# Keys stored a second time in the order of tokens modulo 4, and the triangular products of two heads issued in turn

## The chip, the cores and the metric

One core of a Trainium2 chip runs one program. The metric is device time in microseconds from the program's start to its end; the time of a kernel is the median of its runs.

## What is computed

One decoder layer of 2048 tokens and width 1024, all in float32. Half of the width goes through eight RWKV-7 heads, half through eight attention heads of 64 channels, then an output projection, a layer norm, a mixture of experts and another layer norm. Of this the change touches the attention and the RWKV heads:

```python
DIL_PATTERNS = ((128, 1), (512, 4), (2048, 16))

def dilated_branch(q, k, v, rel_bias, window, dil):
    ...
    def subsample(t):
        t = t.reshape(B, L, dil, H, Dh).transpose(0, 2, 3, 1, 4)
    ...
    logits = jnp.einsum('bdhnqc,bdhnkc->bdhnqk', qs, kb) * (HEAD_DIM ** -0.5) + bias[None, None, :, None]
```

Each head attends three times: in blocks of 128 consecutive tokens, in blocks of 128 tokens that are 4 apart, and in blocks of 128 tokens that are 16 apart. In the first two a block also sees the block before it in the same residue class. The three results are combined by a softmax over their log-sums. The RWKV heads run a recurrence over the tokens, which the kernel computes in chunks of 128 tokens.

## The kernel before

The work runs in stages: `project` (L203) makes all projections, `mixers` (L889) runs RWKV and attention side by side, then come the output projection, the router and the experts. The change touches the first two.

**Projection.** Each product of 128 output channels and 512 tokens is 24 matmuls. For queries and keys (kinds 3 and 4) the sum in PSUM is split into a high part `oh` (L277, ScalarE) and a low part `ol` (L278, VectorE), and both are written to scratch arrays `qs` and `ks` in DRAM (L280) in the order of tokens. The staging tiles have two tags, "a" and "b", of two buffers each. The key chunks are the last that are projected; beside them run the preparation steps of RWKV (`rwkv_prep`, L558), which read and write DRAM too.

**Attention.** `attn_streams` (L968) goes through four head pairs, `hp`, and for each through the patterns n in the order 0, 2, 1. Queries and keys of a head pair lie in two resident tiles, `Q` and `KK`, which `load_qk` (L994) fills in four groups of 512 tokens; `close` (L1017) is called when four blocks are done, loads the values for the next pass and, after the last pattern, the next head pair's queries and keys. A matmul's stationary operand is a block of queries and its moving operand are the keys. `toks` (L1030) gives the access pattern of both: consecutive tokens for n = 0, every 4th word for n = 1, every 16th for n = 2. A block with a block before it needs two products of 256 columns for each head (L1059); one without, a single product that covers high and low part (L1062). Three streams take blocks in turn.

**RWKV.** For 16 rounds and two units each, `rwkv_front` (L648), `rwkv_inverse` (L702) and `rwkv_state` (L799) form triangular products from two heads of 64 channels. The heads lie on partitions 0 to 63 and 64 to 127, so a product of one head uses half of the array's rows. Each writes a PSUM buffer of its own out of the two that a unit has. The helper `triangles` (L643) makes one head's products for a front or an inverse (L646); a state's are made at L818.

**Order.** `weave` (L139) merges the streams by costs written into them as `yield _pe(900)` and the like. The compiler's scheduler then orders each engine's instructions once more by times of its own, so the order of an engine's queue is that of the built program and not that of the lines. An engine works its queue in that order. All loads named here are issued from the queue of SP.

## Time and profile before

| what | value |
|---|---|
| median of 3 runs | 3293.04 us (3287.47 to 3302.23) |
| profiled execution | 3298.42 us, its span 3296.5 us |
| TensorE (PE) busy | 2947.2 us, 89% of the span |
| VectorE (DVE) busy | 2111.6 us, 64% |
| ScalarE (ACT) busy | 1532.7 us, 46% |
| GpSimd (POOL) busy | 674.0 us, 20% |
| DMA | 533.18 MB, mean 162 GB/s |
| chain that ended last | VectorE 1%, issue 1%: the last norm only |

PE is the time of matmuls, PEld that of weight loads, which overlap matmuls. A float32 matmul appears as two records, one of the float32r type as one. The duration of a record covers its whole way through the array, so what a matmul costs its successor is read as the distance between starts. A line such as `L1059 PE MATMUL ... x432 | 115.5, 396 | 14.9` says: 432 records, busy 115.5 us together, 396 ns on average, and 14.9 us of idle time before them, with what ended it. In a timeline the columns are start, length, engine, line, operation, tiles and count, and in brackets the idle time before.

### The profile page before, as it was taken

Reading aid. Unit: us, or ns where it says so; the run is one execution under the profiler, and the core shown is the slowest. Engines: PE = TensorE matmul, PEld = TensorE weight load, DVE = VectorE, ACT = ScalarE, POOL = GpSimd, SP = SyncE. Lnnn points to the kernel's source line nnn. Section 1 sums busy time; section 2 is a strip of 40 time slices with the busy share of each in tenths; the row PEclk is TensorE's granted clock in tenths of the full one; section 3 lists DMA queues with packets and bytes.
Section 4 is the critical chain, followed back from the end, with each engine's and each line's share of the span. In section 5 each row is a group of like instructions: output and inputs, shape, how many; then the busy total and the mean of one; then the engine's idle time right before and its main releaser. Section 6 shows DMA issues by size and latency. Waiting matters only on the chain. (4 is left out here: it accounts for less than half of the span.)

```text
span 3296.5 us, 49200 instructions
## 1 busy us (share of the span) xinstructions
PE 2947.2 (89%) x16686; PEld 2350.5 (71%) x16687; DVE 2111.6 (64%) x4698; ACT 1532.7 (46%) x3650; POOL 674.0 (20%) x673
## 2 busy tenths in 40 slices
PE   7989768999898999998997899899999999998880
PEld 6766656777677777777785677788777777776560
DVE  4997224687555655755748587663577877775756
ACT  3444112465354544444443333411467777765642
POOL 0442000154110212112103122313011111112216
PEclk9999888999889998898997899999999999999895
DMA  5213342598816335235214344233499999996845
GB/s 164 80 58 99 91 73 81 155 287 254 199 45 127 101 84 121 74 78 129 67 38 139 101 150 156 101 136 92 145 309 306 324 314 313 327 300 220 295 128 207
DMA packets 364110, 533.18 MB, mean 162 GB/s; under 512 B 92376, under 2 KB 204736, under 8 KB 363840
## 3 DMA queue, kind: packets, MB, share of 16 engines
q1 hardware_dynamic: 333240, 463.94, 45.0%
q0 software_dynamic: 14208, 45.74, 5.8%
q10 hardware_dynamic: 16408, 20.33, 1.9%
q8 instruction: 134, 2.20, 0.3%
q14 instruction: 120, 0.98, 0.1%
HBM read 402.40 MB, written 128.06 MB: 161 GB/s over the span
## 5 line engine op out<-in xcount | busy, mean ns | idle before, releaser
L1701 DVE TENSOR_TENSOR wl<-raw,wh 128x512 fp32r<-128x512 f32 x768 | 478.1, 682 | 86.3 <-ACT wh L1700 85.8
L1700 ACT CAST wh<-raw 128x512 fp32r<-128x512 f32 x768 | 417.9, 622 | 11.8 <-DMA raw<-in_w_up_dram 10.6
L198 PE MATMUL ps<-xh,wh 128*128 128x512 f32 x640 | 263.4, 412 | 0.4 <-ACT xh L322 0.4
L199 PE MATMUL ps<-xl,wh 128*128 128x512 f32 x640 | 259.6, 406 | 1.0 <-DVE xl L323 1.0
L200 PE MATMUL ps<-xh,wl 128*128 128x512 f32 x640 | 258.7, 404 | 0.0
L1078 ACT ACTIVATE pe<-pe,ms 128x256 f32<-128x256 f32 (+1 forms) x384 | 175.5, 459 | 145.8 <-DVE ms L1075 143.6
L1830 POOL DMA_INDIRECT acc<-ysb,ix x48 | 95.7, 1994 | 624.1 <-ACT ysb L1829 401.7
L198 PE MATMUL pe<-wh,XX 128*128 128x512 f32 x480 | 198.7, 414 | 4.2 <-ACT wh L1700 4.2
L199 PE MATMUL pe<-wl,XX 128*128 128x512 f32 x480 | 191.1, 398 | 2.6 <-DVE wl L1701 2.6
L200 PE MATMUL pe<-wh,XX 128*128 128x512 f32 x480 | 189.7, 395 | 0.0
L198 PEld LDWEIGHTS ps<-xh,wh 128*128 128x128 f32 x640 | 125.3, 196 | 34.3 <-issue 2.8
L199 PEld LDWEIGHTS ps<-xl,wh 128*128 128x128 f32 x640 | 125.2, 196 | 30.3 <-DVE xl L323 2.5
L200 PEld LDWEIGHTS ps<-xh,wl 128*128 128x128 f32 x640 | 124.6, 195 | 29.6
L1098 PE MATMUL po<-pe,V 128*64 128x128 f32 x1200 | 126.0, 308 | 10.7 <-DVE O L1110 7.5
L1059 PE MATMUL pl<-KK,Q 128*128 128x256 f32 x432 | 115.5, 396 | 14.9 <-DMA KK<-ks 6.9
L1084 PE MATMUL pl<-eye,pe 128*128 128x128 f32 x600 | 124.1, 299 | 3.7 <-ACT pe L1078 3.2
L198 PE MATMUL pb<-gh,XH 128*128 128x512 f32 x320 | 126.4, 395 | 0.0
L199 PE MATMUL pb<-gl,XH 128*128 128x512 f32 x320 | 125.6, 392 | 0.0
L200 PE MATMUL pb<-gh,XL 128*128 128x512 f32 x320 | 125.1, 391 | 0.0
L1745 PE MATMUL pe<-wh,XX 128*128 128x512 f32 x288 | 119.7, 416 | 5.4 <-ACT wh L1700 5.4
L198 PE MATMUL pa<-woh,YH 128*128 128x512 f32 x256 | 111.3, 435 | 11.7 <-DVE h L1349 6.8
L1746 PE MATMUL pe<-wl,XX 128*128 128x512 f32 x288 | 118.5, 412 | 2.9 <-DVE wl L1701 2.9
(415 smaller groups left out, 7602.3 us busy)
## 6 DMA issues: line engine op xcount, KB each, us to landing
raw<-in_w_gate_dram SPq DMA_DIRECT2D x128, 512.0 KB
raw<-in_w_up_dram SPq DMA_DIRECT2D x128, 512.0 KB
raw<-in_w_down_dram SPq DMA_DIRECT2D x128, 512.0 KB
pk<-pk SPq DMA_DIRECT2D x32, 512.0 KB
pk_t<-pk SPq DMA_DIRECT2D x32, 512.0 KB
KK<-ks SPq DMA_DIRECT2D x64, 256.0 KB
wr<-in_w_in_dram SPq DMA_DIRECT2D x48, 256.0 KB
rkk<-rkk SPq DMA_DIRECT2D x32, 384.0 KB
```

The lines of the kernel that those rows point to most:

```text
L198: mm(out, lh, rh, start=first, stop=False)
L199: mm(out, lh, rl, start=False, stop=False)
L200: mm(out, ll, rh, start=False, stop=last)
L1059: mm(pl[:, h], q, toks(KK[:, m, h], n, prev, 2), start=m == 0, stop=m == 1)
L1078: nc.scalar.activation(pe[:, h, w], pe[:, h, w], AF.Exp, bias=m_[h], scale=-1.0, accum_out=s_[h])
L1084: nc.tensor.transpose(pt[:, h, b], pe[:, h, b * P:(b + 1) * P], self.c("eye"))
L1098: mm(o[h * 64:(h + 1) * 64, j], vb[:, h * 64:(h + 1) * 64], tt[:, h, b], start=b == kb[0], stop=b == 1)
L1700: nc.scalar.copy(wh[:, c], raw[:, c])
L1701: nc.vector.tensor_tensor(out=wl[:, c], in0=raw[:, c], in1=wh.bitcast(F32)[:, c], op=ALU.subtract)
L1745: mm(ps, L[:, 0:P], wh, start=first, stop=False)
L1746: mm(ps, L[:, 0:P], wl, start=False, stop=last)
L1830: nc.gpsimd.indirect_dma_start(out=self.acc, out_offset=bass.IndirectOffsetOnAxis(ap=ix[0:r, e, b:b + 1], axis=0), in_=ysb[0:r], in_offset ...
```

## The change

Keys (kind 4) are also written to a third array, `ks4`, in which every group of 512 tokens is sorted by token modulo 4: ScalarE copies `oh` and `ol` with a step of 4 into two further tiles of the tags "a" and "b", and each is written with a DMA. After the first pattern of a head pair `close` loads `ks4` over the keys, group by group; the patterns n = 2 and n = 1 read keys from that order (`keys`), with consecutive words for n = 1 and, for n = 2, runs of 32 words with a step of 4. Queries are read as before (`queries`). No product of n = 2 is placed before the first pattern's last group is closed. In the RWKV functions the products of the two heads are written in turn, into two PSUM buffers that are taken together, and the costs given to `weave` change from twice 860, 430 and 900 to once 900, 500 and 950.

```diff
@@ -203,7 +203,8 @@
     def project(self):
         nc, tc, I = self.nc, self.tc, self.I
         x = I["x"][0]
-        self.qs, self.ks = (self.scratch(n, (4, 2, P, S)) for n in ("qs", "ks"))
+
+        self.qs, self.ks, self.ks4 = (self.scratch(n, (4, 2, P, S)) for n in ("qs", "ks", "ks4"))
         self.va = self.scratch("va", (S, DH))
         self.rkk = self.scratch("rkk", (3, DH, S))
         self.rv = self.scratch("rv", (DH, S))
@@ -278,6 +279,11 @@
                         nc.vector.scalar_tensor_tensor(out=ol, in0=ps, scalar=sc, in1=oh.bitcast(F32), op0=ALU.mult, op1=ALU.subtract)
                         for n, o in enumerate((oh, ol)):
                             nc.sync.dma_start((self.qs, self.ks)[kind - 3][cc, n, :, cols], o.bitcast(F32))
+                        if kind == 4:
+                            for n, (o, tag) in enumerate(((oh, "a"), (ol, "b"))):
+                                o4 = st.tile([P, BT], F32, name="o4", tag=tag)
+                                nc.scalar.copy(o4.rearrange("p (d i) -> p d i", d=4), o.bitcast(F32).rearrange("p (i d) -> p d i", d=4))
+                                nc.sync.dma_start(self.ks4[cc, n, :, cols], o4)
                         yield
                         return
                     sh = st.tile([P, BT + 1], F32, name="sh", tag="a")
@@ -640,10 +646,12 @@
         nc.sync.dma_start(v, self.rv[u * P:(u + 1) * P, q * W:(q + 1) * W])
         pp.update(ta=pk[:, 0:W], rt=pk[:, W:2 * W], bk=pk[:, 2 * W:].rearrange("p (c m t) -> p c m t", c=2, m=2), v=v, rho=self.rho[:, u, q])
 
-    def triangles(self, out, pp, h, m):
-        hs = slice(h * 64, (h + 1) * 64)
+    def triangles(self, outs, pp, m):
+
         for c in range(2):
-            self.nc.tensor.matmul(out[:, c], pp["ta"][hs, c * P:(c + 1) * P], pp["bk"][hs, c, m], start=True, stop=True)
+            for h in range(2):
+                hs = slice(h * 64, (h + 1) * 64)
+                self.nc.tensor.matmul(outs[h][:, c], pp["ta"][hs, c * P:(c + 1) * P], pp["bk"][hs, c, m], start=True, stop=True)
 
     def rwkv_front(self, n, pps, last):
 
@@ -655,13 +663,13 @@
         self.busy = True
         C, Dg = T("C", [P, 2, 4, 32], 1), T("Dg", [P, 2, 4, 16], 1)
         AB = T("AB", [P, 2, 2, 2, P], ROUNDS)
+        yield _pe(900)
+        pa = [self.rps[0].tile([P, BT], F32, name="ps0", tag="ps0").rearrange("p (a c s) -> p a c s", a=2, c=2) for _ in range(2)]
+        for i, pp in enumerate(pps):
+            self.triangles([pa[h][:, i] for h in range(2)], pp, 0)
         for h in range(2):
-            yield _pe(860)
-            pa = self.rps[0].tile([P, BT], F32, name="ps0", tag="ps0").rearrange("p (a c s) -> p a c s", a=2, c=2)
-            for i, pp in enumerate(pps):
-                self.triangles(pa[:, i], pp, h, 0)
             yield _dve(4 * P)
-            nc.vector.tensor_tensor(out=AB[:, :, h], in0=pa, in1=self.c("low").unsqueeze(1).unsqueeze(1).to_broadcast([P, 2, 2, P]), op=ALU.mult)
+            nc.vector.tensor_tensor(out=AB[:, :, h], in0=pa[h], in1=self.c("low").unsqueeze(1).unsqueeze(1).to_broadcast([P, 2, 2, P]), op=ALU.mult)
         for i, pp in enumerate(pps):
             pp["AB"] = AB[:, i]
             for d in range(0, P, 32):
@@ -709,12 +717,12 @@
             yield None
         AB, ta = pp["AB"], pp["ta"]
         AW = T("AW", [P, 2, 2, 192])
+        yield _pe(500)
+        pa = [ps()[:, 0:2 * P].rearrange("p (c s) -> p c s", c=2) for _ in range(2)]
+        self.triangles(pa, pp, 1)
         for h in range(2):
-            yield _pe(430)
-            pa = ps()[:, 0:2 * P].rearrange("p (c s) -> p c s", c=2)
-            self.triangles(pa, pp, h, 1)
             yield _dve(2 * P)
-            nc.vector.tensor_tensor(out=AW[:, h, :, 64:192], in0=pa, in1=self.c("low").unsqueeze(1).to_broadcast([P, 2, P]), op=ALU.mult)
+            nc.vector.tensor_tensor(out=AW[:, h, :, 64:192], in0=pa[h], in1=self.c("low").unsqueeze(1).to_broadcast([P, 2, P]), op=ALU.mult)
         yield _pe(215)
         pt = ps()[:, 0:2 * P].rearrange("p (c s) -> p c s", s=P)
         for c in range(2):
@@ -810,12 +818,13 @@
         rt, v = ([pp[m][:, cs] for cs in col] for m in ("rt", "v"))
         bk = [pp["bk"][:, c] for c in range(2)]
         MJ, MK = T("MJ", [P, 2, 2, P]), T("MK", [P, 2, P])
-        for h in range(2):
-            yield _pe(900)
-            pr = ps().rearrange("p (c k s) -> p c k s", c=2, k=2)
-            for c in range(2):
-                for m in range(2):
-                    mm(pr[:, c, m], bk[c][H[h], m], rt[c][H[h]], start=True, stop=True)
+        yield _pe(950)
+        prs = [ps().rearrange("p (c k s) -> p c k s", c=2, k=2) for _ in range(2)]
+        for c in range(2):
+            for m in range(2):
+                for h in range(2):
+                    mm(prs[h][:, c, m], bk[c][H[h], m], rt[c][H[h]], start=True, stop=True)
+        for h, pr in enumerate(prs):
             yield _dve(2 * P)
             nc.vector.tensor_tensor(out=RB[:, h, :, 0:P], in0=pr[:, :, 0, :], in1=self.c("upi").unsqueeze(1).to_broadcast([P, 2, P]), op=ALU.mult)
             yield _dve(2 * P)
@@ -991,13 +1000,15 @@
             skew = src[:, P - 1:P - 1 + P * (L - 1)].rearrange("h (i l) -> i h l", l=L - 1)[:, :, 0:2 * P]
             nc.sync.dma_start(bias[k % 2], skew)
 
-        def load_qk(hp, g):
+        def load_qk(hp, g, ks=None):
+
             cols = slice(g * BT, (g + 1) * BT)
             for n in range(2):
                 half = slice(n * 64, (n + 1) * 64)
-                nc.sync.dma_start(Q[half, :, cols], self.qs[hp, n, :, cols].rearrange("(h c) t -> c h t", h=2))
+                if ks is None:
+                    nc.sync.dma_start(Q[half, :, cols], self.qs[hp, n, :, cols].rearrange("(h c) t -> c h t", h=2))
                 for m in range(2):
-                    nc.sync.dma_start(KK[half, m, :, cols], self.ks[hp, m, :, cols].rearrange("(h c) t -> c h t", h=2))
+                    nc.sync.dma_start(KK[half, m, :, cols], (ks or self.ks)[hp, m, :, cols].rearrange("(h c) t -> c h t", h=2))
 
         def load_v(hp, n, g):
             vcols = slice(hp * P, (hp + 1) * P)
@@ -1024,18 +1035,32 @@
                 load_v(*passes[k + 1], f)
                 if n == 1:
                     load_qk(hp + 1, f)
+                elif n == 0:
+                    load_qk(hp, f, self.ks4)
             if g == 3:
                 load_bias(k + 2)
 
-        def toks(t, n, blk, count):
+        def queries(t, n, blk):
+
+            t = t.bitcast(F32R)
+            if n == 0:
+                return t[..., blk * P:(blk + 1) * P]
+            if n == 1:
+                b, d_ = blk // 4, blk % 4
+                return t[..., b * BT + d_:(b + 1) * BT:4]
+            return t[..., blk::16]
+
+        def keys(t, n, blk, count):
 
             t = t.bitcast(F32R)
             if n == 0:
                 return t[..., blk * P:(blk + count) * P]
             if n == 1:
                 b, d_ = blk // 4, blk % 4
-                return t[..., b * BT + d_:(b + count) * BT:4]
-            return t[..., blk::16]
+                t = t.rearrange("p (b d i) -> p b d i" if len(t.shape) == 2 else "p m (b d i) -> p m b d i", b=4, d=4)
+                return t[:, b:b + count, d_] if len(t.shape) == 4 else t[:, :, b, d_]
+            t = t.rearrange("p m (b d i e) -> p m b d i e", b=4, d=4, e=4)
+            return t[:, :, :, blk % 4, :, blk // 4]
 
         def blocks(s, k):
             hp, n = passes[k]
@@ -1050,16 +1075,20 @@
                 if prev is not None and prev < 0:
                     prev = None
                 two = prev is not None
+                while n == 2 and (hp, 0, 3) not in closed:
+                    yield None
                 yield _pe(450 if two else 230)
                 pl = self.aps.tile([P, 2, 2 * P], F32, name=f"pl{s}", tag=f"pl{s}")
                 for h in range(2):
-                    q = toks(Q[:, h], n, blk, 1)
+                    q = queries(Q[:, h], n, blk)
                     if two:
                         for m in range(2):
-                            mm(pl[:, h], q, toks(KK[:, m, h], n, prev, 2), start=m == 0, stop=m == 1)
+                            kk = keys(KK[:, m, h], n, prev, 2)
+                            mm(pl[:, h].rearrange("p (b i) -> p b i", b=2) if n else pl[:, h], q, kk, start=m == 0, stop=m == 1)
                     else:
 
-                        mm(pl[:, h].rearrange("p (m i) -> p m i", m=2), q, toks(KK[:, :, h], n, blk, 1), start=True, stop=True)
+                        out = pl[:, h].rearrange("p (m i) -> p m i", m=2)
+                        mm(out.rearrange("p m (b i) -> p m b i", b=4) if n == 2 else out, q, keys(KK[:, :, h], n, blk, 1), start=True, stop=True)
                 w = slice(0 if two else P, 2 * P)
                 pe = first(f"pe{s}", [P, 2, 2 * P])
                 if hp not in stats:
```

The built order shows what becomes of this. First, TensorE's queue at a state's triangular products; `ps0_...` are PSUM buffers, one for each head, and each row of `x4` is one head. Before:

```order
L1084 MATMUL pl2_10451<-eye_60,pe2_10393 128x128 x2
L818 MATMUL ps0_9839<-pk_t_9277 128x128 x4
L1098 MATMUL po_7275<-pe0_10076,V_7274 64x128 x2
L1062 MATMUL pl0_10222<-KK_7271,Q_7270 128x256 x2
L818 MATMUL ps0_9859<-pk_t_9277 128x128 x4
L1098 MATMUL po_7275<-pe1_10105,V_7274 64x128 x2
L1062 MATMUL pl1_10309<-KK_7271,Q_7270 128x256 x2
```

and in the changed program:

```order
L826 MATMUL ps0_9982<-pk_t_9452 128x128 x4
L862 MATMUL ps1_10472<-RB1_10137,WF1_10378 64x192 x4
L826 MATMUL ps0_9983<-pk_t_9452 128x128 x4
L879 MATMUL ps1_10522<-vt1_10244,MK1_10139 128x128
L1091 MATMUL pl0_10148<-KK_7368,Q_7367 128x256 x2
L1091 MATMUL pl1_10160<-KK_7368,Q_7367 128x256 x2
L1091 MATMUL pl2_10164<-KK_7368,Q_7367 128x256 x2
```

The two heads stand one after the other with another product between them in both. Of the 32 such places 2 have the heads strictly in turn in the changed program, and 4 more in part.

Second, TensorE's queue where the first head pair passes from n = 0 to n = 2 (key products of a block of n = 0 are the rows with `KK` and x4, those of n = 2 with `KK` and x2; `po` are the products with the values, `pl` with `eye` the transposes, `ps` RWKV). Before:

```order
L1059 MATMUL pl0_7662<-KK_7271,Q_7270 128x256 x4
L1084 MATMUL pl2_7715<-eye_60,pe2_7648 128x128 x2
L1084 MATMUL pl1_7670<-eye_60,pe1_7631 128x128 x4
L1059 MATMUL pl2_7757<-KK_7271,Q_7270 128x256 x4
L1084 MATMUL pl0_7700<-eye_60,pe0_7667 128x128 x2
L1098 MATMUL po_7275<-pe1_7631,V_7274 64x128 x4
L1062 MATMUL pl1_7710<-KK_7271,Q_7270 128x256 x2
L1084 MATMUL pl0_7700<-eye_60,pe0_7667 128x128 x2
L1098 MATMUL po_7275<-pe2_7648,V_7274 64x128 x4
L1062 MATMUL pl0_7748<-KK_7271,Q_7270 128x256 x2
```

and in the changed program:

```order
L1127 MATMUL po_7372<-pe2_7866,V_7371 64x128 x4
L1087 MATMUL pl2_7950<-KK_7368,Q_7367 128x256 x4
L746 MATMUL ps0_7643<-U0_7280,AB_7220 128x128 x4
L1127 MATMUL po_7372<-pe0_7851,V_7371 64x128 x4
L746 MATMUL ps1_7765<-U1_7282,AB_7220 128x128 x4
L752 MATMUL ps0_7689<-t10_7604,X0_7603 128x128 x4
L1113 MATMUL pl2_7982<-eye_60,pe2_7955 128x128 x4
L752 MATMUL ps1_7829<-t11_7685,X1_7684 128x128 x4
L760 MATMUL ps0_7754<-U0_7280,AB_7220 32x32 x8
L1091 MATMUL pl0_8017<-KK_7368,Q_7367 128x256 x2
L1091 MATMUL pl1_8023<-KK_7368,Q_7367 128x256 x2
```

Products of RWKV now stand between the last key product of n = 0 and the first of n = 2.

Third, SP's queue at the same place (`inv` and `Vc` carry the result of an inverse out and back, `V` are values). Before:

```order
L689 DMA inv0_7120<-V64_7109 64x256
L692 DMA Vc_7181<-inv0_7120 128x8x16
L1010 DMA V_7274<-va_71 128x4x128
L992 DMA bias0_7272<-biasrow_2870 128x2x256
L689 DMA inv1_7196<-V64_7109 64x256
L692 DMA Vc_7257<-inv1_7196 128x8x16
L1010 DMA V_7274<-va_71 128x4x128
L675 DMA diag2_7313<-Dg_7316 128x8x16
L679 DMA A64_7108<-diag2_7313 64x256
L1008 DMA V_7274<-va_71 128x4x128
```

and in the changed program:

```order
L697 DMA inv0_7217<-V64_7206 64x256
L1021 DMA V_7371<-va_72 128x4x128
L1011 DMA KK_7368<-ks4_71 64x2x512
L700 DMA Vc_7278<-inv0_7217 128x8x16
L697 DMA inv1_7293<-V64_7206 64x256
L700 DMA Vc_7354<-inv1_7293 128x8x16
L1021 DMA V_7371<-va_72 128x4x128
L1011 DMA KK_7368<-ks4_71 64x2x512 x4
```

The last four key loads (the last row) now stand behind both inverses and a load of values.

## Rows read from the trace of the kernel before

**Rows 1.** Table of stretches: us, busy PE, PEld, DVE, ACT, POOL (records), PEclk, DMA, GB/s

```profile
720.00:845.00 125.00, 120.48 (x503) 91.84 (x501) 86.58 (x209) 64.09 (x166) 53.92 (x70) 0.95 0.83 266
860.00:1720.00 860.00, 818.43 (x6467) 660.99 (x6467) 516.09 (x1943) 421.09 (x1454) 126.52 (x218) 0.91 0.37 89
```

**Rows 2.** Groups by line: key products and triangular products on TensorE

```profile
L1059 PE MATMUL pl<-KK,Q 128*128 128x256 f32 x432 | 115.5, 396 | 14.9 <-DMA KK<-ks 6.9 <-issue 6.3 <-PE po L1098 1.0
L646 PE MATMUL ps<-pk_t 64*128 64x128 f32 x512 | 82.7, 302 | 4.3 <-DVE MK L848 4.1 <-ACT MK L835 0.2
L818 PE MATMUL ps<-pk_t 64*128 64x128 f32 x512 | 74.5, 294 | 6.0 <-DVE MJ L822 4.9 <-DVE S L877 0.8 <-DVE AB L664 0.3
L1062 PE MATMUL pl<-KK,Q 128*128 128x256 f32 x168 | 66.4, 484 | 0.1
```

**Rows 3.** Timeline of TensorE: a chain of n = 0 and the next product

```profile
1102.11 0.74 PE L1059 MATMUL pl<-KK,Q 128*128 128x256 f32 x4
1102.69 0.27 PE L1084 MATMUL pl<-eye,pe 128*128 128x128 f32 x1
```

**Rows 4.** Timeline of TensorE: a chain of n = 1 and the next product

```profile
982.68 1.31 PE L1059 MATMUL pl<-KK,Q 128*128 128x256 f32 x4
983.82 0.51 PE L844 MATMUL ps<-RB,WF 128*128 128x192 f32 x2
```

**Rows 5.** Timeline of TensorE: a pair of n = 2 and the next product

```profile
1103.83 0.77 PE L1062 MATMUL pl<-KK,Q 128*128 128x256 f32 x2
1104.53 0.27 PE L784 MATMUL ps<-t,X 64*64 64x64 f32 x1
```

**Rows 6.** Timeline of the weight loads: first and second of rows 3, then of rows 5

```profile
1102.10 0.54 PEld L1059 LDWEIGHTS pl<-KK,Q 128*128 128x128 f32 x4
1102.21 0.19 PEld L1059 LDWEIGHTS pl<-KK,Q 128*128 128x128 f32 x1
1103.80 0.52 PEld L1062 LDWEIGHTS pl<-KK,Q 128*128 128x128 f32 x2
1104.01 0.31 PEld L1062 LDWEIGHTS pl<-KK,Q 128*128 128x128 f32 x1
```

**Rows 7.** Timeline of TensorE: one head of a state; another state's two heads together

```profile
1223.92 1.16 PE L818 MATMUL ps<-pk_t 64*128 64x128 f32 x8
1225.01 0.65 PE L1098 MATMUL po<-pe,V 128*64 128x128 f32 x6
...
1192.54 1.71 PE L818 MATMUL ps<-pk_t 64*128 64x128 f32 x16
1194.18 0.33 PE L1084 MATMUL pl<-eye,pe 128*128 128x128 f32 x1
```

**Rows 8.** Groups by line from 720 to 845 us: ScalarE's high part

```profile
L277 ACT ACTIVATE oh<-ps 128x512 fp32r<-128x512 f32 x16 | 9.5, 591 | 18.3 <-PE ps L200 9.3 <-issue 8.9
```

**Rows 9.** Timeline of SP at the first hand-off from n = 0 to n = 2

```profile
909.51 0.36 SPq L692 DMA_DIRECT2D Vc<-inv  x1
910.79 0.36 SPq L1010 DMA_DIRECT2D V<-va  x1
```

**Rows 10.** Timelines of SP and TensorE: the first keys' last load, and its user

```profile
850.73 0.59 SPq L1000 DMA_DIRECT2D KK<-ks  x1
...
854.34 0.77 PE L1059 MATMUL pl<-KK,Q 128*128 128x256 f32 x2 [5.16 <-DMA KK<-ks]
```

**Rows 11.** Timeline of TensorE: the first product of n = 2

```profile
899.60 0.81 PE L1062 MATMUL pl<-KK,Q 128*128 128x256 f32 x2
```

**Rows 12.** Timelines of VectorE and TensorE: the first combination of the three patterns

```profile
1068.94 0.19 DVE L1153 TENSOR_TENSOR mn<-stt 128x32 f32<-128x32 f32 x1 [10.93 <-DMA stt<-stat]
...
1069.64 0.69 PE L1098 MATMUL po<-pe,V 128*64 128x128 f32 x4 [7.49 <-DVE O L1110]
```

**Rows 13.** Timeline of TensorE: a wait; and the table of the stretch behind it

```profile
1276.06 1.19 PE L818 MATMUL ps<-pk_t 64*128 64x128 f32 x4 [4.93 <-DVE MJ L822]
...
1276.00:1299.90 23.90, 23.84 (x131) 18.92 (x132) 10.09 (x32) 8.65 (x29) 5.79 (x5) 0.50 0.32 89
```

## The prediction

> **What bounds the kernel now.** I read the table of stretches first. The change lives in two of them: from 720 to 845 us, where the keys are projected, and from 860 to 1720 us, where attention and RWKV share the engines [rows 1]. In the second TensorE is busy 818 of 860 us and VectorE 516, ScalarE 421; its 6,467 matmul records come to 0.127 us each. So a matmul shortened there is worth most of its length, and a wait put into TensorE's queue costs most of its own. In the first TensorE is busy 120 of 125 us, and the DMA engines stand at 0.83 of their time with 266 GB/s, which is 320 GB/s at full share. Then the groups by line give what the change touches: 432 records of two-block key products, 168 of single ones, 512 and 512 of triangular products [rows 2]. Last come single chains in the timeline, because a group's mean says how long a record lies in the pipeline, not how soon the next starts.
>
> **Keys in the order modulo 4.** A chain of four key products of the first pattern goes from 1102.11 to 1102.69: 0.58 us [rows 3]. The same four of the 4-step pattern, where queries and keys are read with a step of 4 words, go from 982.68 to 983.82: 1.14 us [rows 4]. A pair of the 16-step pattern takes 0.70 us [rows 5]. The loads show the stationary half of it: the second load of a contiguous chain starts 0.11 us after the first, that of a strided one 0.21 us after [rows 6]. So 0.58 is one load of 0.11 and four reads of 0.117, and 1.14 is one of 0.21 and four of 0.23, in which the next load runs beside the read. The change makes only the keys (the moving side) contiguous. The queries are the stationary side and keep their steps of 4 and 16. A chain then is 0.21 + 3 x 0.22 (loads) + 0.12 (the last read) = 0.99, a gain of 0.15; a single pair with keys made contiguous gains about as much. From 432 records, 108 chains, 60 belong to the first pattern, so 48 gain 7.2 us, and 16 pairs 2.4 us: **-9.6 us**. For the 16-step pattern the new step of keys is 4 words in runs of 32. 4 words (0.23 a read) and 16 words (0.70 for two, 0.21 + 2 x 0.24) cost the same [rows 4, 5], so I take nothing for its 64 pairs. Bounds: 6 us (only part of the last reads) to 26 us (the load hides wholly: 0.46 in 48 chains, 0.25 in 16 pairs).
>
> The Trainium skill (TensorE: Matmul & The Clock Gate, Part 3, The mechanism) says that a weight load overlaps running matmuls only when its row group is another one. By that rule each contiguous read would be 0.11 us less on the path, 24 us in all. Rows 3 and 6 speak against it: four loads of 0.11 and four reads of 0.117 one after another would be 0.9 us, and the chain took 0.58.
>
> **Alternating heads.** One head's eight records (64 rows of the array) take 1.09 us to the next product. Where both heads happen to follow each other, sixteen take 1.64 instead of 2.18 [rows 7]: part of the second head's records run beside the first's. Full alternation was not seen. Its bounds are 1.09 and 1.64. What counts is the order that was built. Of the 32 products for the states, 4 have both heads adjacent before and 10 after (only 2 strictly alternate); of the 16 fronts 2 and 9; of the 32 sets of the inverse 0 and 7. The rest stand head after head with other work between. So 6 x 0.54 + 7 x 0.54 + 7 x 0.27 (half as many records) + 3 x 0.54 for the three true alternations = **-10.5 us**, bounds 5 and 13. The Trainium skill (TensorEngine Tiling, Theoretical Speedup) gives up to two times for a contraction of 64. By that, alternation everywhere would save 48 x 1.09 + 32 x 0.54 - 3 = 67 us of row 7's prices, which is a rival below, since the built order does not have it.
>
> **Writing the second copy.** 32 ScalarE copies of 128x512, nearest row 0.59 us [rows 8]: 19 us on an engine busy 64 of 125 us; covered, and 19 us at most if not. The 32 writes of 256 KB are 8.4 MB. At 320 GB/s that is 26 us of DMA, and 0.17 x 125 = 21 us are free [rows 1]: **+5 us**, bounds 0 and 26. A late write holds its staging buffer (two per tag), whose next user is the ScalarE copy out of PSUM; five PSUM banks stand between that and TensorE.
>
> **Loading it, four times.** After the first pattern of each head pair the keys of a 512-column group are overwritten, and no product of the second pass may start before the last group has come, since its blocks run over all of them. In the first hand-off the last four loads stand on SP behind a load that waited for the inverse (909.51) and a V load (910.79) [rows 9]. Four issues of 0.59 end near 913; the last key load of the start, issued at 850.73, let TensorE go at 854.34, 3.6 us later [rows 10]. So the keys are there near 917, where the first product of that pass stood at 899.60 [rows 11]: 17 us later. The built order puts 32 products, 64 records, 8 us, in between: **+9 us**. In the other three 54 to 69 products stand between, over 8 us, against 4 x 0.59 + 3.6 = 6 us from the last read of the old keys: covered, but SP holds combine transfers between them, **+4 us** in all, bounds 0 and 30.
>
> A second place: VectorE waits 10.93 us for the statistics of the first head pair, an output copy stands behind that, and TensorE stands 7.49 us behind the copy [rows 12]. In the new order three or four key loads (one 512 KB load before) lie between the statistics' writes and their reading: about 1 us each in three places, **+3 us**, bounds 0 and 10. Lastly the clock: from 1276 us on TensorE, after 4.93 us of waiting, had 0.50 of its clock granted for 24 us [rows 13], the lower of its two levels. Of my new waits the first is as long; a stretch of 8 us at half clock costs **+4 us**, bounds 0 and 20.
>
> **The sum.** 3298.4 (this execution) - 9.6 - 10.5 + 5 + 9 + 4 + 3 + 4 = 3303.3. That execution lies 5.4 above the median of the runs, so 3298 for the median, +0.15%. Between two medians of this kernel about 0.5%, 16.5 us, can be told from no change. **No change** is the forecast, its own range 3282 to 3314.
>
> **Rivals.**
> - The new waits and writes are all covered: 3298.4 - 9.6 - 10.5 - 5.4 = 3273. For it: in three of the four hand-offs the built order has RWKV products ready to fill. Against: the first comes when only 3% of RWKV's products have been placed. Chance 0.17.
> - The key read sets the pace and not the query load: 24 to 26 us instead of 9.6, so 3283. The strided loads of 0.21 speak against it [rows 6]. Chance 0.07. (It is also what the skill's rule on loads would give.)
> - The change does what its words say, and the heads overlap wherever they stand in the new order: 67 instead of 10.5, 3242. Against: where other products stand between the heads, full-array ones among them, one head's eight took 1.09 [rows 7]. Chance 0.06.
> - Slower: the reload gates every hand-off. Eight key and two V loads for the last two groups are 10 x 0.59 + 3.6 = 9.5 us; uncovered four times 38 us instead of 13, with 5 us of lower clock behind each, 20 instead of 4: 3339. It decides as soon as the keys land later than the products placed ahead of the pass. For it: combine transfers that wait for GpSimd stand on SP between the loads. Chance 0.20.
> - The writes are not absorbed, 26 instead of 5: 3319. For it: DMA at 0.83 already. Chance 0.13.
>
> **How the numbers follow.** The forecast has 0.35, so with the second rival no change has 0.42; faster 0.17 + 0.06 + 0.02 left over = 0.25; slower 0.33. The range 3258 to 3338 reaches over the covered case and most of the gated one and leaves out full overlap.
>
> **What would show it.** In the new profile: two-block chains of the 4-step pass near 1.0 us against 1.14 (0.7 would be the second rival), pairs of the 16-step pass still near 0.70; the sixteen triangular records mostly as two runs of 1.09; a wait of TensorE for the key load of 5 to 12 us in the first hand-off, under 3 in the others, where the slower rival has 8 or more; the DMA share from 720 to 845 us near 1, and that stretch at most 10 us longer. The forecast is wrong if the stage from 860 us on changes by more than 20 us.

## The result and the profile after

The changed kernel takes **3368.92 us** (median of 4 runs, 3359.39 to 3378.06) against 3294.64 beside it (4 runs, 3287.47 to 3302.23): ratio 1.0228, 95% interval 1.0208 to 1.0248. It is 74 us slower; 3298 was forecast, and the range ended at 3338. The execution profiled after is the slowest of the four; its span is 3376.0 us, 79.5 more than the one before.

Where the 79.5 us lie, by the start of single products: the first key product moves from 854.34 [rows 10] to 864.90, +10.6. From there to the last product of an RWKV state are 1004.7 us before and 1071.9 after, +67. What follows takes 1437.5 and 1439.2. First the table of stretches: the kernel before from its first key product to its last state, then a fixed stretch, then the first pass of the first head pair from its first to its last key product (columns: window, its length, then busy us and records of PE, PEld, DVE, ACT, POOL, then PEclk, DMA share, GB/s):

```profile
854.30:1859.00 1004.70, 933.55 (x7268) 754.38 (x7268) 611.65 (x2165) 467.86 (x1568) 159.37 (x247) 0.90 0.38 92
850.00:900.00 50.00, 38.87 (x247) 29.59 (x248) 26.28 (x126) 24.51 (x80) 5.26 (x19) 0.80 0.84 173
854.30:898.50 44.20, 37.38 (x236) 28.51 (x236) 24.95 (x121) 23.56 (x78) 3.11 (x11) 0.79 0.83 172
```

The same view of the changed kernel; the first and third rows answer to [rows 1], the fourth is the stage, the fifth the first pass. The last four are the hand-offs, each from the last key product of n = 0 to the first of n = 2:

```profile
720.00:845.00 125.00, 117.46 (x453) 89.37 (x452) 87.41 (x204) 92.08 (x196) 50.16 (x70) 0.90 0.91 300
850.00:900.00 50.00, 27.59 (x166) 22.70 (x163) 12.99 (x44) 13.83 (x41) 7.00 (x29) 0.66 1.07 230
860.00:1720.00 860.00, 771.31 (x5852) 617.39 (x5852) 488.32 (x1820) 381.76 (x1318) 124.55 (x226) 0.85 0.49 110
864.90:1936.80 1071.90, 965.59 (x7291) 774.84 (x7292) 621.95 (x2169) 467.30 (x1568) 164.36 (x268) 0.85 0.45 102
864.90:933.00 68.10, 48.80 (x296) 36.71 (x297) 34.57 (x150) 25.29 (x81) 11.94 (x43) 0.70 0.85 170
933.00:943.00 10.00, 6.28 (x66) 5.75 (x65) 6.95 (x20) 3.37 (x9) 1.51 (x3) 0.98 0.72 164
1148.00:1169.20 21.20, 18.35 (x120) 14.03 (x119) 16.88 (x52) 4.32 (x13) 5.03 (x4) 0.81 0.89 227
1368.00:1389.00 21.00, 16.25 (x124) 13.16 (x122) 9.76 (x25) 6.04 (x17) 6.03 (x5) 0.92 0.93 223
1636.80:1652.60 15.80, 11.68 (x97) 8.81 (x97) 8.71 (x32) 5.01 (x16) 0.88 (x1) 0.93 0.90 224
```

Four things are to be seen. TensorE stands still for 1071.9 - 965.6 = 106 us of the stage, where it was 71: +35. It is busy for 966 us instead of 934: +32, and the two make the 67. Its granted clock is 0.85 instead of 0.90: with two levels that is 30% of the stage at the lower one, 322 us, where it was 201; 121 more cost up to 60. The longer busy time can come from there, since the key products themselves became shorter, as the chains below show. The first pass lasts 68 us instead of 44: +24. And the hand-offs last 9 to 21 us, 66 in all, where the second pass had followed the first within 1.1 us in every head pair. TensorE stands still for 15 us within them; another 13 of the 35 fall into the first pass, 15 into the first passes of the other three pairs, and 7 are saved elsewhere. Part of the hand-offs' time comes back later: the passes of n = 1 take 297 us instead of 311, and what comes behind the attention 6 us less.

The timelines of TensorE, SP and VectorE after show the waits: the first keys, one of RWKV's loads behind them, the last key load of the second hand-off, the first product of the second pass in hand-offs 1 to 4, and the statistics of head pairs 1 and 2, each with TensorE's wait behind it:

```profile
864.90 0.77 PE L1087 MATMUL pl<-KK,Q 128*128 128x256 f32 x2 [7.59 <-DMA KK<-ks]
892.12 0.69 PE L838 MATMUL ps<-eye,v_t 128*128 128x128 f32 x2 [8.88 <-DMA v_t<-rv]
...
1159.91 0.58 SPq L1011 DMA_DIRECT2D KK<-ks  x1
...
942.36 1.04 PE L1091 MATMUL pl<-KK,Q 128*128 128x256 f32 x3 [2.65 <-DMA KK<-ks]
1169.02 1.28 PE L1091 MATMUL pl<-KK,Q 128*128 128x256 f32 x4
1388.61 1.75 PE L1091 MATMUL pl<-KK,Q 128*128 128x256 f32 x6 [1.73 <-issue]
1652.31 1.75 PE L1091 MATMUL pl<-KK,Q 128*128 128x256 f32 x6 [3.73 <-DMA y<-yt]
...
1112.78 0.19 DVE L1182 TENSOR_TENSOR mn<-stt 128x32 f32<-128x32 f32 x1 [15.48 <-DMA stt<-stat]
1114.00 0.48 PE L1113 MATMUL pl<-eye,pe 128*128 128x128 f32 x1 [12.03 <-ACT pe L1107]
1331.59 0.19 DVE L1182 TENSOR_TENSOR mn<-stt 128x32 f32<-128x32 f32 x1 [17.59 <-DMA stt<-stat]
1332.83 1.09 PE L838 MATMUL ps<-eye,pk_t 128*128 128x128 f32 x4 [11.83 <-DVE MJ L831]
```

The direct waits ahead of the second pass are small, and only the first is put down to the reloaded keys by name; the fourth names another transfer. In the second hand-off there is none: 120 records of other work stand ahead of the product, and it comes 9.1 us behind the issue of the last key load (3.6 in [rows 10]). In the four hand-offs that issue comes 2.1, 11.9, 12.8 and 5.1 us behind the last read of the old keys, and the first product of the second pass another 7.2, 9.1, 7.7 and 10.4 us behind the issue.

The chains, on the timeline of TensorE after: one of n = 1 with the next product (answers to [rows 4]), and a pair of n = 2 ([rows 5]):

```profile
1043.89 1.19 PE L1087 MATMUL pl<-KK,Q 128*128 128x256 f32 x4
1044.91 0.38 PE L838 MATMUL ps<-eye,pk_t 128*128 128x128 f32 x2
...
973.55 0.82 PE L1091 MATMUL pl<-KK,Q 128*128 128x256 f32 x2
974.19 0.30 PE L1113 MATMUL pl<-eye,pe 128*128 128x128 f32 x1
```

The chain takes 1.02, the pair 0.64. Over all unbroken ones at the higher clock the medians are: chains of n = 1 1.135 before and 1.049 after (some 30 each), pairs of n = 1 0.659 and 0.583, pairs of n = 2 0.634 and 0.645.

### The profile page after: what moved, and what is told of

The parts are those of the page before. It is cut to its first block, busy times and chain, and to the rows that moved or that the text cites. A ratio compares the mean times of both kernels' runs of the same rounds, so it can differ in the third digit from the quotient of the medians.

```text
span 3376.0 us, 49411 instructions
## 1 busy us (share of the span) xinstructions
PE 2981.1 (88%) x16686; PEld 2374.6 (70%) x16687; DVE 2123.0 (63%) x4698; ACT 1564.0 (46%) x3682; POOL 670.5 (20%) x673
## 5 line engine op out<-in xcount | busy, mean ns | idle before, releaser
L1113 PE MATMUL pl<-eye,pe 128*128 128x128 f32 x600 | 132.2, 313 | 22.8 <-ACT pe L1107 18.8
```

What stands on the lines that cost most here:

```text
L1113: nc.tensor.transpose(pt[:, h, b], pe[:, h, b * P:(b + 1) * P], self.c("eye"))
```

## Experiments: the parts alone

**Theory A**: the loss comes from the second copy of the keys, at the hand-offs and behind the writes, and the lower clock follows the waits. **Rival B**: the triangles, which now hold both heads' PSUM banks at once. **Rival C**: the writes alone.

**Keys alone.** The changed kernel with the triangular products of the kernel before.

> The keys part alone; the triangular products stand head after head as before. Theory A (hand-offs): nearly all of the loss comes from the second copy of the keys. The pass that follows the first pattern starts 9 to 21 us late in each of four hand-offs, the attention begins about 10 us late, its first pass lasts 24 us longer, and TensorE is at the lower clock behind these waits: 3355 to 3375 us, over 60 above the kernel before. Rival B (PSUM banks): holding both heads' banks of a triangular product at once delays the chains behind it, and the keys cost 20 us or less: 3300 to 3320.

Measured 3354.7 (4 runs), ratio 1.0193 (1.0159 to 1.0226), +59. B falls as the main cause.

**Triangles alone.** The cut shows the state's products; the helper `triangles` and the costs given to `weave` change as in the change.

```diff
-        for h in range(2):
-            pr = ps()...
-            for c, m: mm(pr[:, c, m], bk[c][H[h], m], rt[c][H[h]])
+        prs = [ps()... for _ in range(2)]
+        for c, m:
+            for h in range(2): mm(prs[h][:, c, m], bk[c][H[h], m], rt[c][H[h]])
```

> The triangles part alone; keys as before. Theory A: within 12 us of the kernel before, 3283 to 3300, since the built order rarely alternates heads. Rival B: 3340 to 3355, most of the loss being here. By the prediction's own term it would be 10.5 us faster, 5 to 13.

Measured 3295.57 (10 runs), 1.0002 (0.9983 to 1.0021): no change. The groups by line show why: 79.1 and 72.2 us busy, against 82.7 and 74.5 [rows 2].

```profile
L648 PE MATMUL ps<-pk_t 64*128 64x128 f32 x512 | 79.1, 305 | 0.4 <-DVE Q L863 0.3
L820 PE MATMUL ps<-pk_t 64*128 64x128 f32 x512 | 72.2, 301 | 0.0
```

**The reload alone.**

```diff
+                elif n == 0:
+                    load_qk(hp, f, self.ks)        # the natural copy again
+                while n == 2 and (hp, 0, 3) not in closed:
+                    yield None
```

> The kernel before, with the keys loaded a second time behind the first pattern, at the place and with the gate of the change, but from the same natural copy: no second copy is written, and products read as before. Theory A: the four hand-offs alone cost 9 to 21 us each less what the stages catch up, with the lower clock behind them: 3330 to 3350, 35 to 55 above before. Rival C (writes): the second copy's 8.4 MB and the late start cause the loss, and the reload costs under 20: 3300 to 3315.

Measured 3353.21 (4 runs), 1.0188 (1.0155 to 1.0221), +57. C falls as the only cause: the reload costs by itself what the whole keys part does. Its stage is 1058.4 us long, with 0.86 of the clock.

**The writes alone.** The copies and writes of the changed kernel in the kernel before; nothing reads them.

> The kernel before with the second copy made and written, and never read. The prediction had 5 us, 0 to 26. Theory A: the 8.4 MB push the first loads of the attention back by about 10 us, of which part is taken up by RWKV's products: 5 to 15 above before. If the difference between keys alone (59 above) and reload alone (57 above) is the writes less the 9.6 of the keys: 12 above. If the DMA engines take them in their free time: 0 to 3 above.

Measured 3334.91 (4 runs), 1.012 (1.0102 to 1.0138), +37. All three expectations, up to 15, were too low. So both parts are large alone, and 37 + 57 do not add up to 59. Why is open: a late first pass does not cover its own reload, for in the profiles the first hand-off of the keys alone lasts 14.2 us and that of the reload alone 11.2. In the profiled execution, 31 us above before, the first product starts 9.3 us later and the first pass lasts 57.2 us instead of 44.1. The first product, on the timeline:

```profile
863.59 0.77 PE L1064 MATMUL pl<-KK,Q 128*128 128x256 f32 x2 [10.04 <-DMA KK<-ks]
```

## Experiments: what in each part

**The copies without the writes.** The line that stores the second copy is taken out.

> The writes' 32 ScalarE copies into the shared staging tiles, and no write behind them. If the rest of the writes' loss (17 of 37 us with a quarter of the bytes) is the copies themselves, 10 to 20 above before; if it is the writes that hold the two staging tiles of a tag and the issues on SP, 0 to 6 above.

Measured 3301.67 (10 runs), 1.0014 (0.9992 to 1.0036), +5 and not clear of noise. The ScalarE copies are covered, or nearly.

**A quarter of the bytes.**

```diff
-    nc.sync.dma_start(self.ks4[cc, n, :, cols], o4)
+    nc.sync.dma_start(self.ks4[cc, n, :, tb * BT:tb * BT + P], o4[:, 0:P])
```

> As the run with the writes alone (3335, 37 above before): the same 32 copies, staging tiles and 32 issues, but each write takes only the first 128 of 512 columns, 2.1 MB instead of 8.4. If the bytes cost (DMA engines full from 700 to 900 us, the first loads behind them): a quarter of the loss or less, 0 to 12 above before. If the copies, the shared staging tiles or the issues cost: 25 or more above.

Measured 3312.02 (10 runs), 1.0047 (1.0031 to 1.0063), +17: between the two. The stretches of the profiled execution, the slowest of the ten:

```profile
720.00:845.00 125.00, 118.87 (x479) 90.92 (x478) 88.03 (x213) 94.22 (x203) 54.30 (x71) 0.95 0.85 268
850.00:900.00 50.00, 30.68 (x175) 24.19 (x177) 15.69 (x58) 16.54 (x49) 7.27 (x30) 0.66 1.05 209
```

In the first the DMA engines are back at 0.85 and 268 GB/s, as before the change. Still the second stays at 30.7 us of TensorE. The projection shows what is left. The first and the last write of the keys' natural copy on SP, before, with the whole second copy, and with a quarter of it:

```profile
721.65 0.32 SPq L280 DMA_DIRECT2D ks<-oh  x1
843.75 0.38 SPq L280 DMA_DIRECT2D ks<-ol  x1
...
722.04 0.32 SPq L280 DMA_DIRECT2D ks<-oh  x1
856.07 0.34 SPq L280 DMA_DIRECT2D ks<-ol  x1
...
725.58 0.32 SPq L280 DMA_DIRECT2D ks<-oh  x1
854.07 0.34 SPq L280 DMA_DIRECT2D ks<-ol  x1
```

That is 122.1, 134.0 and 128.5 us, and 120.0 with the copies alone. With a quarter of the bytes about half of the delay is left, as of the loss: it does not go with the bytes alone. The waits of ScalarE and of VectorE in this run from 720 to 870 us name writes that hold the staging tiles; with the copies alone neither row is there (columns: waiting line, releaser, us, times, longest).

```profile
ACT oh L277 <- DMA ks<-oh: 4.9, 1, 4.9
...
DVE ol L278 <- DMA ks<-ol: 9.1, 1, 9.1
```

Whether the held tiles alone make the delay, or the 32 further issues on SP and their packets as well, was not separated: a quarter of the bytes still makes 4,610 more packets than before, as many as the whole writes.

**The gate alone.** The two lines with `while n == 2`, no reload.

> The kernel before with the gate alone: no block of the second pass is put into the order before the last output copy of the first pattern is; nothing is written or loaded again. If the reload's wait for its transfers makes the loss of the hand-offs: 0 to 8 above before. If holding back the second pass by itself empties TensorE's order at the hand-off: 20 or more above; the half reload (48 above, where the full one has 57) would then be explained.

Measured 3299.54 (10 runs), 1.0029 (1.0006 to 1.0053), +5. Its hand-offs last 1.1, 0.1, 0.1 and 3.1 us: so the longer ones come from the reload and not from the gate.

**Half of the reload.** Only the high halves are loaded again: `for m in range(2 if ks is None else 1)`.

> As the run with the reload alone (3353, 57 above before), but only the high halves of the keys are loaded again: 16 issues instead of 32 in a hand-off's set and 1 MB instead of 2 per hand-off from the last close of 0.5, half in all; the gate stays. If the transfer of the bytes and the issues set the wait, about half of the loss stays: 20 to 35 above before, and the gaps ahead of the second pass go from 11 to 20 us to 6 to 12. If the gate alone or the latency of the last load sets it, 45 or more above before.

Measured 3345.55 (4 runs), 1.0161 (1.0136 to 1.0187), +48. The four hand-offs come to 5.9, 10.5, 10.3 and 13.7 us, 40 in all, against 11.2, 13.3, 19.2 and 19.6, 63 in all, of the whole reload. The profiled execution, 3334.72, is the fastest of the four, 36 above the one before, where that of the whole reload has 48. So the hand-offs follow the transfers, and the total does not follow them in proportion: the expectation of 20 to 35 failed. (The whole reload is 16 loads of 256 KB in each hand-off, 16.8 MB in all, and this run half of it; the expectations of this run and the next count 32 loads and 8 MB.)

**The reload issued earlier.** Each group of keys is loaded again right behind the last product that reads it.

> The reload alone (3353, 57 above), but each group of keys is loaded again right behind the last product that reads it, where the change waits for the output copies of the group after it; the gate opens with the last of these loads. If the place of the issue is the larger part of the wait (the last issue came 3 to 12 us behind the last read), the gaps go from 11 to 20 us to 5 to 10 and the loss to 20 to 40. If the 8 MB themselves and what they meet on the DMA engines make it, 45 or more above before.

Measured 3339.62 (4 runs), 1.0115 (1.0084 to 1.0147), +43. The hand-offs stay at 12.0, 20.7, 13.4 and 13.5 us, so the place of the issue in the program is not what makes them long. On SP the last load still comes 3.8 to 12.8 us behind the last read, since inverses and, in later pairs, the combination's transfers stand between. Why the total fell by a quarter is open.

**Work put into the hand-offs.**

```diff
+                for _ in range(24 if n == 2 and blk < 3 else 0):
+                    mm(pl[:, 0], Q[:, 0, 0:P]..., Q[:, 1, 0:2 * P]..., start=True, stop=True)
```

> As the run with the reload alone (3353), with 24 further products of 256 columns, over queries already there, ahead of the first product of each stream in the second pass, so that TensorE has work where it waited for the keys: 72 products in a hand-off, some 9 to 17 us. If the lower clock behind the gaps is a large part of the loss, the time at half clock (259 us in the mixers' stage, 155 before) falls by 40 or more and the kernel comes out 5 to 20 us below 3353. If the waiting alone costs, it stays or gets up to 20 slower.

Measured 3367.95 (4 runs), 1.0238 (1.0201 to 1.0276), 15 above the reload. The stage of the reload, then the stage with the added products and their group:

```profile
850.10:1908.50 1058.40, 960.57 (x7268) 778.41 (x7268) 614.10 (x2165) 470.13 (x1568) 156.39 (x247) 0.86 0.45 103
```

```profile
854.90:1917.90 1063.00, 978.19 (x7555) 792.01 (x7556) 614.64 (x2165) 465.50 (x1568) 158.16 (x247) 0.89 0.45 102
...
L1062 PE MATMUL pl<-Q 128*128 128x256 f32 x288 | 47.1, 299 | 0.0
```

The clock rises from 0.86 to 0.89: 296 us at the lower level become 234, worth up to 31. 288 products, 47.1 us busy, lengthen the stage by 4.6 only: without them TensorE is busy 931 us where the reload has 961, 30 less. The time at the lower level in the hand-offs and the second passes behind them is 37 us before, 119 with the reload and 31 with the fill. So the lower clock is a real price of the hand-offs, some 30 us, and the fill pays for it with as much; the 5 to 20 us below the reload, which were expected, did not come.

## Experiments: what the two ideas are worth

**Alternation held by ordering edges**, without the second copy.

```diff
-            for h in range(2):
-                mm(prs[h][:, c, m], ...)
+            for h in (1, 0):
+                prev = self.behind(prev, mm(prs[h][:, c, m], ...))
```

`behind` adds an edge that keeps the issue order of two products and makes no wait; head 1 now comes first in each pair.

> The triangles part alone, with the order on TensorE held by ordering edges: of each set the products of head 1 and head 0 follow each other strictly, and in the built order over 80% of the neighbours in a set are of the other head (13% in the change). If two 64-row products of different heads run at once, sixteen records take 1.1 us (less where the upper bound of 2.2 stood), so 40 to 67 us less: 3230 to 3255. If they overlap only partly, as where head followed head (1.64 against 2.18), 25 to 35 less: 3260 to 3270. If alternation gives nothing, or the chain behind the products and not TensorE sets the pace, 3285 to 3300.

Measured 3269.71 (5 runs), 0.992 (0.9896 to 0.9945), **26 us faster**. The timeline and the groups:

```profile
951.59 1.16 PE L828 MATMUL ps<-pk_t 64*128 64x128 f32 x16
952.68 0.79 PE L1073 MATMUL pl<-KK,Q 128*128 128x256 f32 x2
...
L648 PE MATMUL ps<-pk_t 64*128 64x128 f32 x512 | 62.9, 316 | 3.3 <-DVE MK L859 2.3 <-DVE S L888 0.6 <-ACT MK L846 0.2
L828 PE MATMUL ps<-pk_t 64*128 64x128 f32 x512 | 55.2, 309 | 8.8 <-DVE S L888 7.7 <-ACT yt L896 1.1
```

Sixteen records of two heads take 1.09 us, what eight of one head took [rows 7]: the second head is free. The groups fall by 157.2 - 118.1 = 39 us and not by half: of the 48 sets of sixteen only seven stand unbroken at the higher clock. Many are split, with fourteen records in 1.09 us and the other two placed elsewhere, where they take 0.42. The stage of this run (columns as above):

```profile
856.70:1836.70 980.00, 889.35 (x7275) 707.01 (x7276) 610.07 (x2166) 463.41 (x1568) 154.65 (x239) 0.90 0.39 94
```

TensorE is busy 44 us less than before and stands still 19 us more, 90.6 instead of 71.2. Its waits for VectorE come to 53 us, where they were 36: that is where a good part of what the products gain goes.

**The same in the change.**

> The change itself with the alternation held by ordering edges. If the two parts add up: 3369 - 26 = 3343, 3335 to 3350. If the waits at the hand-offs hide what TensorE gains: 3355 to 3370.

Measured 3316.09 (10 runs), 1.0049 (1.0028 to 1.007): 53 below the change, twice what it gave alone and less than either expectation. Its stage stands still as long as the change's, 109 against 106 us, with a clock of 0.88 instead of 0.85. Why the clock stays higher is open.

**No step in any read.**

```diff
-                return t[..., b * BT + d_:(b + count) * BT:4]
-            return t[..., blk::16]
+                return t[..., b * BT + d_ * P:b * BT + (d_ + 1) * P] if count == 1 else t[..., b * BT:b * BT + 2 * P]
+            return t[..., blk * P:(blk + 1) * P]
```

> The kernel before, with queries and keys of the second and third pattern read without a step, from the columns of the first pattern: it works on other tokens, and only the time counts. By the prediction's mechanism (the strided query load of 0.21 sets the pace once the keys are contiguous) the four-record chains of the 4-step pattern go from 1.14 to about 0.58 us, pairs of the other from 0.70 to 0.35: 48 x 0.56 + 16 x 0.35 + 64 x 0.35 = 55 us at most, so 3240 to 3265. If the stage is bound by the chain of the engines behind the products and not by them: under 15 us less.

Measured 3254.5 (4 runs), 0.9895 (0.9859 to 0.9931), 40 us faster. A chain and a pair on its timeline:

```profile
984.84 0.74 PE L1059 MATMUL pl<-KK,Q 128*128 128x256 f32 x4
985.42 0.38 PE L1084 MATMUL pl<-eye,pe 128*128 128x128 f32 x2
...
920.03 0.50 PE L1062 MATMUL pl<-KK,Q 128*128 128x256 f32 x2
920.37 0.65 PE L793 MATMUL ps<-AW,U 128*128 128x192 f32 x3
```

With both sides contiguous the chain takes 0.58 and the pair 0.34; with the keys contiguous for n = 1 alone 1.02 and, where both still have a step, 0.64. Once the keys are contiguous, the query load sets the pace.

**One copy of the keys.** Stored modulo 4 only and read so by all three patterns; in the first, bias columns and V rows take the same order.

> Keys stored once, by token modulo 4, and read so by all three patterns: no second copy, no reload, no gate; the first pattern works on its keys in that order (its bias columns and V rows follow, by 8 ScalarE copies and 48 further V issues). The triangles are those of the kernel before. Term of the prediction for the keys: 9.6 us faster, 6 to 26, so 3270 to 3290; if the contiguous read gains nothing that reaches the end of the kernel, 3292 to 3300; if the additional V issues delay the loads, above 3300.

Measured 3301.55 (10 runs), 1.0011 (0.9999 to 1.0024): nothing gained. In the profiled execution the stage is 6 us shorter than before, 998.6 against 1004.7, but begins 3 us later, and what follows it takes 6 us more.

**One copy and held alternation.**

> The one copy of the keys together with the ordered alternation of the heads, a candidate that keeps both ideas of the change and drops the reload. If both gains add: 3296 - 26 (measured for the alternation) - 6 to 26 (keys) = 3244 to 3264. If they compete for the same time, or the V issues cost, 3265 to 3285.

Measured **3242.9** (4 runs), 0.9845 (0.9821 to 0.9869). It is 55 us faster than the kernel before and 126 faster than the change, the fastest of all runs here. Its stage (same columns):

```profile
860.00:1802.90 942.90, 869.90 (x7276) 697.29 (x7276) 609.19 (x2166) 466.44 (x1574) 156.58 (x242) 0.92 0.40 98
```

Alone the parts gave -26 and +4. Its clock is 0.92, where the alternation alone has 0.90; 0.02 of 943 us is 19. The stage is 37 us shorter than that of the alternation alone: 19 are busy time and 18 standing still. Why the two together hold the clock up and shorten the waits is open.

## Why the prediction was wrong

No change was forecast, and the kernel became 74 us slower. Three steps failed: the writes were put into the free share of the DMA engines, the hand-offs were taken as covered wherever RWKV's products fill them, and the lower clock was priced once. By term:

- **Keys, -9.6**: the mechanism was right (the strided query load paces; pairs of n = 2 stay), the size too large. Medians give 48 x 0.086 + 16 x 0.076 = 5.3 us, below the lower bound of 6, and nothing of it reached the end of the kernel in the one-copy run. The rule of the Trainium skill (TensorE: Matmul & The Clock Gate, Part 3, The mechanism) that a load overlaps a running matmul only where the row group differs does not fit here either: four contiguous reads and four loads took 0.58 in the run without steps. The same section also has loads into a background weight buffer pulled ahead; these rows would fit that, but no run here shows where a load goes.
- **Alternation, -10.5**: alone it gave 0 (-6 to +7). What was counted in the order, sets that stand head behind head, brought 5.9 us of busy time in the groups and none in the end. The rival of full alternation was right on the products (1.09 for sixteen) and too large in the sum: -26 instead of -67 where edges hold the order. Split sets leave 39 of the 67 in the groups, and TensorE stands still 19 us longer. The factor of two that the Trainium skill gives for a contraction of 64 (TensorEngine Tiling, Theoretical Speedup) is what those sixteen show.
- **Writes, +5, bounds 0 to 26**: measured 37 alone. The failed step is the free share: 0.17 x 125 us was taken as room. The stretch took 300 instead of 266 GB/s, 34 x 125 us = 4.3 MB more, where 8.4 were added. So some 4 MB, 14 us at 300 GB/s, were pushed behind it, beside the attention's first loads and RWKV's, which the prediction did not look at: DMA share 1.07 from 850 to 900 us, TensorE 27.6 of 50 us busy. The second step that failed is that a held staging tile is far from TensorE: with a quarter of the bytes, when the share is 0.85 again, the key writes still take 6 us longer than before and the kernel loses 17. That the tiles make this delay is argued from their waits. In the change the start came 10.6 us later and the first pass took 24 more. The copies were covered, as said.
- **Reload, +13**: measured 57 alone. TensorE's standing still in the hand-offs is close to the term, 15 us in the change and 21 with the reload alone. The waits ahead of the second pass were not where they were said: 2.65 us in the first hand-off (5 to 12 said), up to 3.7 in the others (under 3). The failed step is "covered": a hand-off was priced by the wait alone, and 6 us were given from the last read to the keys. The second pass came 9 to 21 us behind that read, with the last issue up to 12.8 us late. RWKV's products that fill this time were taken as free. In the second hand-off 120 records fill 21.2 us, 0.177 a record against 0.127 [rows 1], with 2.9 us of standing still and a clock of 0.81. What was done there is only in part saved later: 66 us of hand-offs against some 23 in later stretches. The second passes themselves wait no more than before, under 2 us in all. The gating rival (3339) had the place right, and 38 us of waits for what showed up as longer hand-offs.
- **Statistics, +3, bounds 0 to 10**: TensorE waits 12.03, 11.83 and 7.28 us behind them, 31.1 in all, where 7.49, 4.93 and 7.54 were before, 20.0 in all: +11. It is not the key loads alone: with the gate and no reload these waits were 9.09, 7.67 and 10.01 us.
- **Clock, +4, bounds 0 to 20**: the worst in proportion. 121 us more at the lower level are up to 60 us; the fill run prices the reload's share at about 30. The prediction priced one stretch of 8 us. In the change the four hand-offs and the second passes behind them have 101 us at the lower level, where 37 were before.
- **Signs**: of those named, the chains and the DMA share (0.91) did not speak against the forecast, and the waits missed their values by little; only the length of the stage from 860 us on, over 20 us more, called it clearly wrong.

What of the 14 us between the change and its keys part alone is due to the triangles' order isn't settled; holding that order takes away more than these.

## What to carry to other kernels

Here a stretch whose DMA engines were 0.83 busy did not take 8 MB more for nothing: ask which loads stand behind them, and which tiles a late write holds. A wait that other work covers is not free either. Price three things: the time in which the engine stands still, what the later stretches give back of the work that was put ahead, and the granted clock in and behind each gap. The length of the hand-offs alone does not tell: half of the reload cut it from 63 to 40 us and the loss from 57 to 48 only. When an order matters, as between two heads' products, hold it by edges; writing the loops in that order did nothing here.

## What was not expected of the hardware

- Products of 64 rows on different halves of the array ran wholly side by side: sixteen records in 1.09 us alternating, 1.64 where one head follows the other, and 1.09 for each head where they stand apart [rows 7].
- TensorE's granted clock fell to 0.50 also where the trace shows no idle time in the 8.4 us ahead. Stretches of the changed kernel inside a pass of n = 2, the second at the lower level throughout, with TensorE busy in every microsecond of both:

```profile
1180.00:1188.40 8.40, 8.40 (x73) 6.66 (x72) 4.90 (x18) 4.34 (x19) 0.00 (x0) 1.00 0.06 20
1188.40:1208.90 20.50, 20.50 (x138) 16.68 (x136) 6.64 (x25) 8.65 (x34) 2.68 (x9) 0.50 0.07 20
```
